# A two-layer trunk kernel on one core: from the framework's instruction scheduler to one written in the kernel

## The chip, the cores and the metric

The kernel runs on one core of a Trainium2 chip. The time is device time in microseconds (us) of one launch, lower is better. The engines of the core are named as in the profile: PE (TensorE, the matrix engine), DVE (VectorE), ACT (ScalarE), POOL (GpSimd) and SP (SyncE, which here issues every DMA). Each engine runs its own list of instructions strictly in order, and waits at an instruction until what that instruction needs is there.

## The reference

One sequence of 512 frames with 1024 features, led by 112 zero pads and 16 meta tokens, passes two layers and a last norm. Everything is float32.

```python
h = concat([zeros(112), meta_tokens(16), x(512)])          # 640 x 1024
# layer 0: w_in_ab (1024 x 4184)
aq, ak, av, ag, iq, ik, iw, bq, bk, bv, bg, ba = split(rms_norm(h, g0) @ w_in_ab)
oa = dsa_attention(...)       # indexer scores, top 128 keys of each query, softmax with a bias table
ob = gla_chunked(...)         # gated linear attention in chunks of 64
h += concat([oa * silu(ag), head_rms(ob) * silu(bg)]) @ w_out_ab
# layer 1: w_in_cd (1024 x 3584)
cq, ck, cv, cg, dq, dk, dv, dg = split(rms_norm(h, g1) @ w_in_cd)
oc = retention_chunked(rotary(cq), rotary(ck), cv)
od = stick_breaking(dq, dk, dv)      # softplus, reversed running sum, exp, times values
h += concat([head_layer_norm(oc) * silu(cg), od * silu(dg)]) @ w_out_cd
y = rms_norm(h[128:], final_g)
```

## The kernel before, in words

All state stays on the chip: the normalized sequence is held feature-major (128 features on the partitions, 528 positions: 16 meta tokens and 512 frames), and every projection is a sum over eight blocks of 128 features into a PSUM tile `acc` (two of them). To reach float32 accuracy each operand is split in two parts that the matrix engine takes: `hi` (line 135, on ACT) rounds it, `lo` (line 141, on DVE unless told otherwise) takes the remainder. A product is three matmuls (line 247): first part by first, second by first, first by second. The activations' parts are `hh` and `hl`, the weights' `wh` and `wl`.

Weights stream in. `load` (line 198) issues the DMA of the next 128x512 tile `raw` on SP; `split_next` makes `wh` on ACT and `wl` on DVE or, for three tiles in eight (`WPOOL = 3`), on POOL; five tiles are in flight. `COMB` is a projection whose weights are gathered from three places by three DMAs a half, over a tile that POOL zeroes first.

The projections are the matrix engine's stream, and everything else is laid beside them. Each branch is a Python generator (attention, the linear-attention heads, `stick_steps` at line 1220 and on, `retention_steps`, the norm) that does a little and yields; `tick` advances these generators between the products of a projection, with lags set by `LAG`. So the order in which the program states its work is already interleaved: `L1` and `L2` list the branches, V values, G linear attention, D the end of the top-k selection, A sparse attention, C its gate, S stick-breaking, R retention.

In the stick-breaking steps the chain of one unit is: scores on PE (line 460, `s`), a copy to SBUF (line 1246, DVE), absolute value, exp and log on ACT, a reversed running sum (line 1255, `TENSOR_TENSOR_SCAN`, DVE), a difference (1257, DVE), exp (1258, ACT), four transposes on PE (line 294, `tr<-ident,wt`), and the split of the turned tile into `pt` (135 on ACT, 141 on DVE) for the product with the values.

The order of the instructions on each engine is made by the framework's scheduler, which takes the program in the stated order and fills buffers with its own cost model; only `load_x`, the first stage, stands exactly as written (`manual_schedule`). Three PSUM banks serve both `s` and `tr` (the pool named `x` in the changed kernel), one serves `pv` (`y`), and rings of 8 and 10 SBUF buffers serve the tiles `st` and `wt`.

Of the kernel before, what the change touches and what calls it, by code (L numbers as in the profile page):

```python
# [9 lines left out]
F32 = mybir.dt.float32  # L10
# [6 lines left out]
P = 128  # L17
# [4 lines left out]
T = NMETA + SEQ  # L22
# [12 lines left out]
SROW = 656  # L35
# [4 lines left out]
    return slice(NMETA + P * b, NMETA + P * (b + 1))  # L40


class Kernel:
    def __init__(self, ctx, tc, ins, out):
        self.ctx, self.tc, self.nc = ctx, tc, tc.nc
        self.ins, self.out = ins, out
        nc = self.nc
        pool = lambda name, **k: ctx.enter_context(tc.tile_pool(name=name, bufs=1, **k))
# [5 lines left out]
        self.pp = pool("psum", space=bass.MemoryType.PSUM)  # L54
        self.dp = pool("scratch", space=bass.MemoryType.DRAM)
# [51 lines left out]
        return self.sm.tile(shape, F32, tag="mid", bufs=4, name=self.name("mid"))  # L107


    ST, WT, PT, GT = 8, 10, 8, 2  # L110
    RAW, WB = 5, 5


    WEVERY, WAHEAD, WPOOL = 1, 2, 3

    NL = (2, 5)

# [142 lines left out]
    def add(self, steps, wait=1, name=None):  # L260
        self.chains.append([self.now + wait, steps, name])
# [35 lines left out]
    def consts(self):  # L297
        nc, ins = self.nc, self.ins
        nc.scalar.preload_act_table_set("natural_log_exp_and_others")
        self.ident = self.cp.tile([P, P], F32, name="ident")  # L300
        make_identity(nc, self.ident)
# [46 lines left out]
    def load_x(self):  # L348
# [198 lines left out]
    def bias_steps(self):  # L547
        nc, ins = self.nc, self.ins
        rb = self.cp.tile([32, 8], F32, name="rb")
        nc.sync.dma_start(rb, ins["rel_bias"])  # L550
        oh = self.wt()
        oh2 = self.wt()
        nc.sync.dma_start(oh[:32, :512], ins["c_bucket"][:, :512])
        nc.sync.dma_start(oh2[:32, :SROW - 512], ins["c_bucket"][:, 512:])
        self.reps = []
        yield 8
        s1, s2 = self.s(), self.s()
        nc.tensor.matmul(s1[:8, :512], rb, oh[:32, :512], start=True, stop=True)
        nc.tensor.matmul(s2[:8, :SROW - 512], rb, oh2[:32, :SROW - 512], start=True, stop=True)
        r = self.wt()  # L560
        r2 = self.wt()
        nc.vector.tensor_copy(r[:8, :512], s1[:8, :512])
        nc.vector.tensor_copy(r2[:8, :SROW - 512], s2[:8, :SROW - 512])
        self.rows = self.dp.tile([8, SROW], F32, name="rows")
        nc.sync.dma_start(self.rows[:, :512], r[:8, :512])
        nc.sync.dma_start(self.rows[:, 512:], r2[:8, :SROW - 512])
        for h in range(8):
            t = self.dp.tile([P, SROW], F32, name=f"rep{h}")
            row = self.rows[h:h + 1, :]
            nc.sync.dma_start(t, bass.AP(tensor=row.tensor, offset=row.offset, ap=[[0, P], [1, SROW]]))  # L570
            self.reps.append(t)
        yield 1

    def strip(self, h):
        t = self.lt()
        row = self.reps[h][0:1, :]
        src = bass.AP(tensor=row.tensor, offset=row.offset + P - 1, ap=[[SROW - 1, P], [1, T]])
        self.nc.sync.dma_start(t, src)
        return t

# [752 lines left out]
    def play(self, parts, run):  # L1333
        for p in parts.split():
            run[p[0]](*(int(x) for x in p[1:]))

    def run(self):
        nc = self.nc
        self.consts()
        with self.tc.manual_schedule(engines={e.engine for e in (nc.tensor, nc.vector, nc.scalar, nc.gpsimd)}):  # L1340
            a, b = self.load_x()
        self.late_consts()
        self.add(self.bias_steps())
        self.indexer(a, b)
# [12 lines left out]
@with_exitstack  # L1357
# [63 lines left out]
```

## Time and profile before

| | us |
|---|---|
| median of three timed runs | 687.61 (687.45 to 688.51) |
| the profiled execution, its own time | 686.27 |
| its span, first to last instruction | 684.5 |
| PE busy in it | 644.6 (94%) |
| DVE busy | 485.1 (71%) |
| ACT busy | 386.1 (56%) |
| POOL busy | 150.9 (22%) |

The profile is of one execution. Times in it are in us from the start of the span. The stages, read off the first and last instruction of their lines: start and first norm 0 to 25, indexer and top-k with the values and the linear attention beside it 25 to 187, sparse attention 187 to 312, out-projection of layer 0 and the norm and values of layer 1 to 425, stick-breaking heads S0 and S1 425 to 486, retention R0 486 to 538, S2 and S3 538 to 600, R1 600 to 633, the last out-projection 633 to the end. An idle time that is put down to an engine's line is the time for which the waiting instruction's engine did nothing until that line's result came.

### The profile page before, as it was taken

To read this page: it belongs to the slowest core of one execution; us is meant where nothing else is said; L and a number is where in the kernel's file an instruction comes from. 1 tells how busy PE (TensorE), PEld (TensorE's weight loads), DVE (VectorE), ACT (ScalarE), POOL (GpSimd) and SP (SyncE) were. 2 spreads that over 40 slices of the span, in tenths; PEclk is the share of its full clock that TensorE was granted. 3 is DMA by queue.
4 is the path that set the end of the run, shared out by engine and by line. 5 is a ranking of instruction groups with operands and counts; after the bars stand their busy time and mean duration, and the time that the engine had idled before them with its cause. 6 is when DMAs were issued, how large, how long until landed. Compare 5 with 4: busy or idle time off the path is not lost.

```text
span 684.5 us, 12281 instructions
## 1 busy us (share of the span) xinstructions
PE 644.6 (94%) x4469; PEld 584.6 (85%) x4469; DVE 485.1 (71%) x1216; ACT 386.1 (56%) x846; POOL 150.9 (22%) x181
## 2 busy tenths in 40 slices
PE   8999998999999999999999999898899989799996
PEld 7879998989899999988898898777788778688784
DVE  5667899999968788798414635979635788935633
ACT  5656554252445747585435655888443798544434
POOL 6302211131131111020332221111221111310240
PEclk9999999999999999999999999999999999999999
DMA  8446223123124132112242642122222221313503
GB/s 231 109 106 200 60 59 93 47 79 104 36 80 110 47 94 63 47 48 78 79 126 60 200 126 78 32 77 62 63 63 66 58 62 47 94 47 97 186 25 123
DMA packets 91103, 59.25 MB, mean 87 GB/s; under 512 B 7314, under 2 KB 81628, under 8 KB 91044
## 3 DMA queue, kind: packets, MB, share of 16 engines
q1 hardware_dynamic: 91044, 58.48, 29.7%
q8 instruction: 35, 0.57, 0.3%
q14 instruction: 24, 0.20, 0.1%
HBM read 53.18 MB, written 6.90 MB: 88 GB/s over the span
## 4 chain that ended last, share of the span: by engine, by line
PE 54%; DVE 31%; ACT 10%; issue 3%; POOL 1%; DMA 0%; SPq 0%; ACTq 0%; DVEq 0%
PE acc L247 32%; PE tr L294 4%; DVE wt L1255 3%; PE acc L1295 3%; DVE m L536 3%; DVE lt L537 3%; DVE wl L141 3%; PE s L1295 2%; ACT st L135 2%; DVE wt L1257 1%; PE pv L683 1%; PE pv L684 1%; DVE wt L1091 1%; PE s L460 1%; DVE wt L1246 1%
## 5 line engine op out<-in xcount | busy, mean ns | idle before, releaser
L247 PE MATMUL acc<-hh,wh 128*128 128x272 f32 (+2 forms) x968 | 249.2, 317 | 3.0 <-ACT wt L610 1.0
L247 PE MATMUL acc<-hh,wl 128*128 128x272 f32 (+2 forms) x968 | 234.6, 302 | 1.3 <-POOL wl L141 1.3
L247 PE MATMUL acc<-hl,wh 128*128 128x272 f32 (+2 forms) x968 | 234.3, 303 | 0.7 <-DVE hl L143 0.7
L247 PEld LDWEIGHTS acc<-hh,wh 128*128 128x128 f32 x968 | 159.5, 191 | 11.9 <-issue 1.6
L135 ACT ACTIVATE wh<-raw 128x512 fp32r<-128x512 f32 x152 | 95.2, 628 | 131.1 <-PE acc L247 94.5
L247 PEld LDWEIGHTS acc<-hh,wl 128*128 128x128 f32 x968 | 159.0, 190 | 7.7 <-POOL wl L141 1.5
L247 PEld LDWEIGHTS acc<-hl,wh 128*128 128x128 f32 x968 | 158.6, 190 | 3.9 <-DVE hl L143 1.1
L141 POOL TENSOR_TENSOR wl<-raw,wh 128x512 fp32r<-128x512 f32 x58 | 76.1, 1311 | 344.2 <-ACT wh L135 314.4
L141 DVE TENSOR_TENSOR wl<-raw,wh 128x512 fp32r<-128x512 f32 x96 | 70.9, 741 | 37.0 <-ACT wh L135 32.8
L294 PE MATMUL tr<-ident,wt 128*128 128x128 f32 (+2 forms) x300 | 48.6, 282 | 10.1 <-DVE pt L141 5.9
L294 PEld LDWEIGHTS tr<-ident,wt 128*128 128x128 f32 (+2 forms) x300 | 35.1, 142 | 16.7 <-DVE pt L141 7.5
L460 PE MATMUL s<-st,st 128*128 128x272 f32 (+4 forms) x128 | 37.4, 304 | 5.3 <-DVE wt L1246 2.2
L135 ACT ACTIVATE st<-acc 64x528 fp32r<-64x528 f32 (+1 forms) x58 | 34.8, 599 | 1.7 <-PE acc L247 0.7
L747 POOL TENSOR_TENSOR gt<-gt,wt 128x528 f32<-128x528 f32 (+1 forms) x16 | 22.3, 1396 | 59.5 <-ACT wt L746 53.3
L460 PEld LDWEIGHTS s<-st,st 128*128 128x128 f32 x128 | 24.1, 188 | 11.9 <-issue 3.9
L537 DVE MATCH_REPLACE8 lt<-m,lt 128x144 f32<-128x144 f32 (+1 forms) x64 | 31.2, 492 | 0.1
L141 DVE TENSOR_TENSOR pt<-tr,pt 128x384 fp32r<-128x384 f32 (+1 forms) x48 | 27.9, 595 | 3.9 <-ACT pt L135 3.7
L1255 DVE TENSOR_TENSOR_SCAN wt<-wt,wt 128x144 f32<-128x144 f32 (+3 forms) x32 | 29.5, 942 | 1.6 <-ACT wt L1251 1.3
L536 DVE MAX8 m<-lt 128x8 f32<-128x144 f32 (+1 forms) x64 | 30.1, 498 | 0.6 <-POOL lt L530 0.4
L803 ACT ACTIVATE wt<-wt,tiny 128x144 f32<-128x144 f32 (+3 forms) x32 | 18.2, 571 | 19.4 <-DVE tiny L800 16.7
L683 PE MATMUL pv<-pt,vt 128*128 128x256 f32 x96 | 27.1, 283 | 0.0
L684 PE MATMUL pv<-pt,vt 128*128 128x256 f32 x96 | 26.9, 280 | 0.0
(247 smaller groups left out, 1093.7 us busy)
## 6 DMA issues: line engine op xcount, KB each, us to landing
raw<-in_w_in_ab_dram SPq DMA_DIRECT2D x64, 256.0 KB, 2.8
raw<-in_w_in_cd_dram SPq DMA_DIRECT2D x56, 256.0 KB, 2.9
raw<-in_w_out_ab_dram SPq DMA_DIRECT2D x16, 256.0 KB, 2.7
raw<-in_w_out_cd_dram SPq DMA_DIRECT2D x16, 256.0 KB, 2.6
rep<-rows SPq DMA_DIRECT2D x8, 328.0 KB, 6.9
lt<-rep SPq DMA_DIRECT2D x8, 264.0 KB, 2.9
pt<-in_x_dram SPq DMA_DIRECT2D x8, 256.0 KB, 4.4
wt<-in_x_dram SPq DMA_DIRECT2D x8, 256.0 KB, 4.0
```

What stands on the lines that cost most here:

```text
L135: self.nc.scalar.activation(out, src, AF.Copy, scale=1.0 if scale is None else scale)
L141: (eng or nc.vector).tensor_tensor(out, src, h, op=ALU.subtract)
L247: nc.tensor.matmul(a[:, c.start - c0:c.stop - c0], w[:, k % 4, :], x[:, k, c], start=k == order[0] and i == 0, stop=k == order[-1] and i == 2)
L294: self.nc.tensor.transpose(out, in_, self.ident[p0:p0 + n, p0:p0 + n])
L460: nc.tensor.matmul(out, q[:, qs], k[:, ks], start=True, stop=False)
L536: nc.vector.max(m8, sc)
L537: nc.vector.match_replace(sc, m8, sc, MARK)
L683: nc.tensor.matmul(dst, xh, pl, start=False, stop=False)
L684: nc.tensor.matmul(dst, xl, ph, start=False, stop=last and i == len(parts) - 1)
L747: nc.gpsimd.tensor_tensor(t[:, c], t[:, c], e[:, c], op=ALU.mult)
L1255: nc.vector.tensor_tensor_scan(mv[:, ::-1], mv[:, ::-1], lv[:, ::-1], 0.0, ALU.add, ALU.add)
L1295: nc.tensor.matmul(o[b], m[:, k, blk(b)], x, start=k == order[0] and i == 0, stop=k == order[-1] and i == 2)
```

## The change

The kernel's methods call the same instructions in the same stated order, but on recorders in place of the engines and the tile pools. `Recorder.add` notes each instruction with what it reads and writes, and gives it a cost from a table of fitted durations (`price`). After the whole program is recorded, `order` places all instructions with a list scheduler: in a loop, it offers for each engine one instruction that is ready (the one whose inputs come soonest, and of those that are there in time the one stated first; for PE an instruction counts as in time only when its inputs were there 300 ns before PE is free), takes the engine whose offer starts first, and gives out the buffers of each tag in the stated order. `issue` then emits the result with all five engines under `manual_schedule`, SP's DMAs among them.

Beside that, `WPOOL` goes from 3 to 0: all second parts `wl` but one go to DVE (57 instructions leave POOL), the rings grow (`st` 8 to 10, `wt` 10 to 12, `gt` 2 to 4), and the program is built with a smaller scratch for DMA descriptors. The arithmetic and the number of matmuls stay.

```diff
+    def add(self, eng, name, args, kw):
...
+        o.at = o.pri = len(self.ops)
...
+        for write, xs in ((False, ins), (True, outs)):
+            for x in xs:
+                self.depend(o, x, write)
+        self.price(o)
+        self.ops.append(o)
...
+    def price(self, o):
...
+        if o.eng == "tensor":
...
+            o.cost = max(273, 170 + 0.4375 * n) if not two else 180 + 1.62 * n
+        elif o.eng == "scalar":
+            o.cost = (205 if sbuf else 165) + 0.83 * n + (80 if isinstance(o.kw.get("bias"), View) or isinstance(o.kw.get("scale"), View) else 0)
...
+        elif o.eng == "vector":
+            o.port = sbuf and o.name not in ("max", "match_replace")
+            if o.name == "tensor_tensor_scan":
+                o.cost = 144 + 2.1 * n
...
+            else:
+                o.cost = 148 + 1.05 * n + scalar
...
+        elif o.eng == "gpsimd":
+            o.cost = {"memset": 92 + 0.84 * n, "tensor_tensor": 178 + 2.17 * n}.get(o.name, 194 + 1.5 * n)
+        else:
...
+            o.cost = 2000 + kb * (9 if any(y.tile.whole for y in o.outs + o.ins) else 3.5)
+    LAT = {"tensor": 55, "vector": 33, "scalar": 34, "gpsimd": 60, "sync": 27}
+    OVER = {"vector": -84, "scalar": -103, "gpsimd": -60}
+    SWITCH, ROWS = 86, 50
+    MARGIN = 300
...
+    def order(self):
...
+        while left:
+            best = None
+            for e, xs in lists.items():
+                pick = None
+                base = free[e] + (last.mm[2] if e == "tensor" and last is not None else 0)
+                for o in xs:
+                    est = o.est
+                    ok = True
+                    for t in o.tiles:
+                        if t.slot:
+                            continue
+                        k = t.kind
+                        if t.at != k.next or not k.free:
+                            ok = False
+                            break
+                        est = max(est, min(k.free)[0] + self.LAT[e])
+                    if not ok:
+                        continue
+                    now = free[e] + (self.slot(last, o) if e == "tensor" and last is not None else 0)
+                    start = max(est, now)
+                    key = (max(est + (self.MARGIN if e == "tensor" else 0) - base, 0.0), o.pri)
+                    if pick is None or key < pick[0]:
+                        pick = (key, start, o)
+                if pick and (best is None or pick[1] < best[1]):
+                    best = pick
...
+            if e == "vector" and o.port and begun.get("pool", (0, 0))[0] < start < begun.get("pool", (0, 0))[1] - 100:
+                cost += begun["pool"][1] - start - 70
...
+    def issue(self):
+        todo = self.order()
...
+        with self.tc.manual_schedule(engines=engines):
+            for o in todo:
...
+                getattr(getattr(self.core, o.eng), o.name)(*[bind(x) for x in o.args],
+                                                           **{k: bind(x) for k, x in o.kw.items()})
...
-    ST, WT, PT, GT = 8, 10, 8, 2
-    RAW, WB = 5, 5
+    ST = 10
+    WT = 12
+    PT = 8
+    GT = 4
...
-    WEVERY, WAHEAD, WPOOL = 1, 2, 3
+    WPOOL = 0
...
-        with self.tc.manual_schedule(engines={e.engine for e in (nc.tensor, nc.vector, nc.scalar, nc.gpsimd)}):
-            a, b = self.load_x()
+        a, b = self.load_x()
...
+        nc.issue()
...
+                     dynamic_dma_scratch_size=1024)
```

In the changed kernel every instruction is issued from line 373, so its rows all show that line. PE before, at the end of S1, near 484 us: `acc_1201` is the value projection of R0, `tr_1215` the bank into which the last unit's weights (`wt_1186`) are turned.

```order
3107 L247 MATMUL acc_1201_6373<-hh_799_4221,wl_1190_6307 128x272
3108 L247 MATMUL acc_1201_6373<-hh_799_4221,wl_1190_6307 128x256
3109 L294 MATMUL tr_1215_6451<-ident_76,wt_1160_6174 128x128
3110 L294 MATMUL tr_1205_6404<-ident_76,pm_1146_6105 32x128
3111 L294 MATMUL tr_1215_6451<-ident_76,wt_1186_6293 128x128
3112 L294 MATMUL tr_1215_6451<-ident_76,wt_1160_6174 128x128
3113 L294 MATMUL tr_1215_6451<-ident_76,wt_1186_6293 128x128
3114 L247 MATMUL acc_1201_6373<-hh_799_4221,wh_1189_6306 128x272
```

PE in the changed kernel at the same place: `acc_58` is the gate projection that follows that value projection, `x_238` the bank of the same transposes, `wt_195` the last unit's weights.

```order
3127 L373 MATMUL acc_58_6463<-hl_3_4254,wh_110_6196 128x512
3128 L373 MATMUL acc_58_6463<-hh_3_4242,wl_110_6253 128x512
3129 L373 MATMUL acc_58_6463<-hh_3_4242,wh_111_6242 128x512
3130 L373 MATMUL x_238_6497<-ident_76,wt_187_6291 128x128
3131 L373 MATMUL x_238_6497<-ident_76,wt_195_6420 128x128
3132 L373 MATMUL x_238_6497<-ident_76,wt_187_6291 128x128
3133 L373 MATMUL x_238_6497<-ident_76,wt_195_6420 128x128
3134 L373 MATMUL x_235_6366<-ident_76,pm_7_6235 32x128
3135 L373 MATMUL acc_58_6463<-hl_3_4254,wh_111_6242 128x512
```

The last part of the value projection and the first part of the gate's, 25 matmuls, now stand ahead of the last unit's transposes. Near the end of S3 it is the same with the projections of R1.

ACT before, in the first norm: `hh` are the first parts of the first blocks of the sequence, made of the turned input `s`.

```order
12 L135 ACTIVATE hh_2_135<-s_39_221,gains_132 128x272
13 L135 ACTIVATE hh_2_135<-s_40_227,gains_132 128x272
14 L135 ACTIVATE hh_2_135<-s_42_234,gains_132 128x272
15 L377 ACTIVATE wt_44_241,tiny_43_240<-pt_13_156 128x512
16 L135 ACTIVATE hh_2_135<-s_46_249,gains_132 128x272
```

ACT in the changed kernel at the same place: `wh_4` and `wh_5` are the first parts of the two halves of `COMB`, made of `raw_4` and `raw_5`.

```order
15 L373 ACTIVATE hh_2_324<-x_4_272,gains_84 128x272
16 L373 ACTIVATE hh_2_324<-x_5_274,gains_84 128x272
17 L373 ACTIVATE tiny_9_315<-tiny_9_315,eps_83 128x1
18 L373 ACTIVATE tiny_9_315<-tiny_9_315 128x1
19 L373 ACTIVATE wh_4_347<-raw_4_232 128x512
20 L373 ACTIVATE wh_5_357<-raw_5_242 128x512
21 L373 ACTIVATE hh_2_324<-x_6_351,gains_84 128x272
22 L373 ACTIVATE hh_2_324<-x_7_360,gains_84 128x272
```

Two splits of weights now stand ahead of the fourth and later `hh`.

SP in the changed kernel, where the DMAs of those two tiles stand among the constants (before, the three DMAs of each tile stood together, ahead of all constants):

```order
18 L373 DMA w2_98<-in_gla_gate_w2_dram 16x256
19 L373 DMA tri_99<-in_c_tri_dram 128x128
20 L373 DMA strict_100<-in_c_strict_dram 128x128
21 L373 DMA raw_4_232<-in_w_in_ab_dram 128x4x8
22 L373 DMA raw_5_242<-in_w_in_ab_dram 128x4x8
23 L373 DMA dmat_101<-in_c_dmat_dram 128x512
24 L373 DMA raw_7_309<-in_w_in_ab_dram 128x4x128
25 L373 DMA zeta_102<-in_c_zeta_dram 128x8
26 L373 DMA raw_4_232<-in_w_in_ab_dram 128x4x16
27 L373 DMA raw_5_242<-in_w_in_ab_dram 128x4x16
```

The third DMA of each tile has moved behind five DMAs of constants and two other weight tiles.

## Rows read from the trace of the kernel before

**Rows 1.** Page, busy time: engine, us, share of the span, instructions
```profile
PE 644.6 (94%) x4469; PEld 584.6 (85%) x4469; DVE 485.1 (71%) x1216; ACT 386.1 (56%) x846; POOL 150.9 (22%) x181
```

**Rows 2.** Windows: stretch, length, PE, PEld, DVE, ACT, POOL busy, clock, DMA, GB/s
```profile
75.00:187.00 112.00, 106.21 (x833) 101.06 (x832) 108.09 (x334) 48.47 (x111) 23.37 (x33) 0.98 0.27 69
187.00:312.00 125.00, 121.04 (x969) 116.76 (x968) 101.17 (x324) 78.31 (x182) 22.57 (x20) 1.00 0.25 67
...
425.00:486.00 61.00, 53.56 (x340) 45.39 (x339) 55.65 (x115) 48.14 (x96) 13.57 (x11) 0.99 0.23 66
486.00:538.00 52.00, 52.00 (x327) 45.49 (x327) 22.94 (x42) 23.66 (x48) 7.66 (x6) 0.98 0.21 59
538.00:600.00 62.00, 54.29 (x343) 46.17 (x342) 56.18 (x117) 48.69 (x99) 13.26 (x11) 0.98 0.21 62
```

**Rows 3.** Waits of PE, 425 to 600: us in total, times, longest
```profile
PE tr L294 <- DVE pt L141: 5.1, 2, 2.7
PE tr L294 <- DVE wt L1246: 3.6, 6, 1.2
...
PE s L460 <- DVE pt L141: 1.3, 4, 0.4
```

**Rows 4.** Timeline, two ends of a stick stretch: start, us, engine, instruction, [idle before]
```profile
480.35 1.58 POOL L141 TENSOR_TENSOR wl<-raw,wh 128x512 fp32r<-128x512 f32 x1 [1.07 <-ACT wh L135]
480.72 2.33 DVE L1255 TENSOR_TENSOR_SCAN wt<-wt,wt 128x528 f32<-128x528 f32 x1
...
484.91 0.48 PE L294 MATMUL tr<-ident,wt 128*128 128x128 f32 x1 [2.35 <-DVE pt L141]
...
594.30 1.25 DVE L1255 TENSOR_TENSOR_SCAN wt<-wt,wt 128x528 f32<-128x528 f32 x1
```

**Rows 5.** Timeline of PE, two neighbours of a projection
```profile
429.74 0.40 PE L247 MATMUL acc<-hl,wh 128*128 128x512 f32 x1
429.98 0.39 PE L247 MATMUL acc<-hh,wl 128*128 128x512 f32 x1
```

**Rows 6.** Window of 3.4 us behind a stall of PE (columns as rows 2)
```profile
597.30:600.70 3.40, 3.18 (x15) 2.89 (x15) 2.27 (x6) 2.47 (x6) 0.61 (x1) 0.50 0.00 0
```

**Rows 7.** Instructions on `wl`: page (POOL), line 141 (DVE, min/median/max ns)
```profile
L141 POOL TENSOR_TENSOR wl<-raw,wh 128x512 fp32r<-128x512 f32 x58 | 76.1, 1311 | 344.2 <-ACT wh L135 314.4
...
L141 DVE TENSOR_TENSOR wl<-raw,wh x96: 655/691/1725, 18.3 to 664.8; 128x512 fp32r<-128x512 f32 x96
```

**Rows 8.** Windows, `wl` on POOL alone: stretch, length, POOL busy (x)
```profile
75.00:187.00 112.00, 12.13 (x10) 0.98 0.27 69
187.00:312.00 125.00, 13.40 (x11) 1.00 0.25 67
425.00:486.00 61.00, 6.86 (x5) 0.99 0.23 66
```

**Rows 9.** Waits of PE, 75 to 312
```profile
PE tr L294 <- DVE attm L969: 3.1, 3, 2.0
...
PE tr L294 <- DVE tiny L791: 0.8, 2, 0.5
```

**Rows 10.** Waits of PE, 312 to 425
```profile
PE tr L294 <- ACT wt L1116: 1.3, 2, 0.7
```

**Rows 11.** Last selection step, first step of attention that uses it: min/median/max, first, last start
```profile
L536 DVE MAX8 m<-lt x64: 280/495/712, 74.4 to 186.7; 128x8 f32<-128x144 f32 x16, 128x8 f32<-128x272 f32 x16, 128x8 f32<-128x400 f32 x16, 128x8 f32<-128x528 f32 x16
...
L785 DVE TENSOR_TENSOR wt<-lt,lt x32: 286/501/1659, 202.1 to 313.7; 128x144 f32<-128x144 f32 x8, 128x272 f32<-128x272 f32 x8, 128x400 f32<-128x400 f32 x8, 128x528 f32<-128x528 f32 x8
```

**Rows 12.** Timeline of the start, ACT and SP's queue
```profile
13.88 0.49 ACT L135 ACTIVATE hh<-s,gains 128x272 fp32r<-128x272 f32 x1 [1.66 <-PE s L294]
...
18.89 0.63 ACT L135 ACTIVATE wh<-raw 128x512 fp32r<-128x512 f32 x1
...
15.49 0.43 SPq L320 DMA_DIRECT2D zeta<-in_c_zeta_dram  x1
```

**Rows 13.** Page, DMA issues: KB each, us from issue to landing
```profile
raw<-in_w_in_ab_dram SPq DMA_DIRECT2D x64, 256.0 KB, 2.8
```

More of the change, by code (lines that the diff above doesn't have):

```diff
@@ L40, in blk, with __init__, __getitem__, __getattr__ @@
     return slice(NMETA + P * b, NMETA + P * (b + 1))
+class View:
+    __slots__ = ("tile", "chain", "real")
+    def __init__(self, tile, chain, real):
+        self.tile, self.chain, self.real = tile, chain, real
+    def __getitem__(self, k):
+        return View(self.tile, self.chain + (("__getitem__", (k,), {}),), self.real[k])
+    def __getattr__(self, name):
+        got = getattr(self.real, name)
+        if name not in ("rearrange", "unsqueeze", "broadcast_to", "bitcast"):
+            return got
+        return lambda *a, **k: View(self.tile, self.chain + ((name, a, k),), got(*a, **k))
+    def other(self, fn):
+        return View(self.tile, (("", fn, None),), fn(self.real))
+    def bind(self):
+        x = self.tile.shaped(self.tile.buf)
+        for name, a, k in self.chain:
+            x = a(x) if name == "" else getattr(x, name)(*a, **k)
+        return x
+    def region(self):
+        t = self.tile
+        if t.whole:
+            return 0, 1, 0, 1
+        x = self.real
+        ap, off = [list(y) for y in x.ap], x.offset
+        width = t.width
+        p0, c0 = off // width, off % width
+        lo = c0 + sum(min(0, st * (n - 1)) for st, n in ap[1:])
+        hi = c0 + sum(max(0, st * (n - 1)) for st, n in ap[1:]) + 1
+        if t.psum:
+            return 0, P, 0, t.width
+        return p0, p0 + ap[0][1], lo, hi
+    def free(self):
+        n = 1
+        for y in self.real.shape[1:]:
+            n *= y
+        return n
@@ new lines, with __init__, shaped @@
+class Held:
+    def __init__(self, kind, shape, dt, psum, whole):
+        self.kind, self.shape, self.dt, self.psum, self.whole = kind, list(shape), dt, psum, whole
+        self.buf, self.slot, self.left, self.ends = None, None, 0, 0.0
+        self.log, self.fixed = [], False
+    def shaped(self, buf):
+        if self.fixed:
+            return buf
+        n = 1
+        for y in self.shape[1:]:
+            n *= y
+        x = buf[:self.shape[0], :n]
+        if x.dtype != self.dt:
+            x = x.bitcast(self.dt)
+        if len(self.shape) > 2:
+            names = "abcd"[:len(self.shape) - 1]
+            x = x.rearrange(f"p ({' '.join(names)}) -> p {' '.join(names)}", **dict(zip(names, self.shape[1:])))
+        return x
@@ new lines, with __init__, buffer, tile @@
+class Kind:
+    def __init__(self):
+        self.free, self.made, self.next, self.n = [], 0, 0, 0
+    def buffer(self, i, dt):
+        self.n += 1
+        return self.pool.tile([P, self.width], dt, tag=f"{self.tag}_{i}", bufs=1, name=f"{self.tag}_{self.n}")
+class RecordedPool:
+    def __init__(self, rec, pool, psum=False, whole=False):
+        self.rec, self.pool, self.psum, self.whole = rec, pool, psum, whole
+        self.kinds = {}
+    def tile(self, shape, dt, tag=None, bufs=1, name=None):
+        fixed = tag is None
+        tag = tag or name
+        n = 1
+        for y in shape[1:]:
+            n *= y
+        if tag not in self.kinds:
+            k = self.kinds[tag] = Kind()
+            width = max(n, {"tiny": 32, "mid": P}.get(tag, 0))
+            k.width, k.pool, k.tag = width, self.pool, tag
+            k.free = [(0.0, i) for i in range(bufs)]
+            k.any = self.pool.tile(shape, dt, name=tag) if fixed else k.buffer(0, F32)
+        k = self.kinds[tag]
+        t = Held(k, shape, dt, self.psum, self.whole)
+        t.width = k.width
+        if fixed:
+            t.fixed, t.buf = True, k.any
+        return View(t, (), t.shaped(k.any))
@@ new lines, with __init__, __getattr__ @@
+class Op:
+    __slots__ = ("eng", "name", "args", "kw", "outs", "ins", "tiles", "preds", "succs", "wait", "est", "at", "cost",
+                 "mm", "port", "pri", "begin", "end")
+class RecordedEngine:
+    def __init__(self, rec, name, engine):
+        self._rec, self._name, self._engine = rec, name, engine
+    def __getattr__(self, op):
+        if op in ("preload_act_table_set", "engine"):
+            return getattr(self._engine, op)
+        return lambda *a, **k: self._rec.add(self._name, op, a, k)
@@ L43 @@
 class Kernel:
     def __init__(self, ctx, tc, ins, out):
-        self.ctx, self.tc, self.nc = ctx, tc, tc.nc
+        self.ctx, self.tc, self.nc = ctx, tc, Recorder(tc)
         self.ins, self.out = ins, out
         nc = self.nc
-        pool = lambda name, **k: ctx.enter_context(tc.tile_pool(name=name, bufs=1, **k))
+        pool = lambda name, psum=False, whole=False, **k: RecordedPool(
+            self.nc, ctx.enter_context(tc.tile_pool(name=name, bufs=1, **k)), psum, whole)
         self.cp = pool("const")
@@ L53, in __init__ @@
         self.sm = pool("small")
-        self.pp = pool("psum", space=bass.MemoryType.PSUM)
-        self.dp = pool("scratch", space=bass.MemoryType.DRAM)
+        self.pp = pool("psum", True, space=bass.MemoryType.PSUM)
+        self.dp = pool("scratch", False, True, space=bass.MemoryType.DRAM)
         self.n = 0
@@ L107, in mid @@
         return self.sm.tile(shape, F32, tag="mid", bufs=4, name=self.name("mid"))
-    ST, WT, PT, GT = 8, 10, 8, 2
-    RAW, WB = 5, 5
-    WEVERY, WAHEAD, WPOOL = 1, 2, 3
+    ST = 10
+    WT = 12
+    PT = 8
+    GT = 4
+    RAW = 5
+    WB = 5
+    WEVERY = 1
+    WAHEAD = 2
+    WPOOL = 0
     NL = (2, 5)
@@ L300, in consts @@
         self.ident = self.cp.tile([P, P], F32, name="ident")
-        make_identity(nc, self.ident)
+        make_identity(nc.core, self.ident.real)
         warm = self.pv()
@@ L568, in bias_steps @@
             t = self.dp.tile([P, SROW], F32, name=f"rep{h}")
-            row = self.rows[h:h + 1, :]
-            nc.sync.dma_start(t, bass.AP(tensor=row.tensor, offset=row.offset, ap=[[0, P], [1, SROW]]))
+            nc.sync.dma_start(t, self.rows.other(lambda x, h=h: bass.AP(
+                tensor=x[h:h + 1, :].tensor, offset=x[h:h + 1, :].offset, ap=[[0, P], [1, SROW]])))
             self.reps.append(t)
@@ L575, in strip @@
         t = self.lt()
-        row = self.reps[h][0:1, :]
-        src = bass.AP(tensor=row.tensor, offset=row.offset + P - 1, ap=[[SROW - 1, P], [1, T]])
+        src = self.reps[h].other(lambda x: bass.AP(
+            tensor=x[0:1, :].tensor, offset=x[0:1, :].offset + P - 1, ap=[[SROW - 1, P], [1, T]]))
         self.nc.sync.dma_start(t, src)
@@ L1408 @@
     from concourse.bass_utils import run_bass_kernel_spmd as _run
-    nc = _bacc.Bacc("TRN2", target_bir_lowering=False, num_devices=1)
+    nc = _bacc.Bacc("TRN2", target_bir_lowering=False, num_devices=1,
+                     dynamic_dma_scratch_size=1024)
     arrays, aps = {}, {}
```

138 lines of the change are left out of this document (added).

## The prediction

> **What bounds the kernel now.** I read the busy times first. PE is busy for 644.6 of 684.5 us, and no other engine comes near it [rows 1]. The number of matmuls stays, so the change can only win what PE does not work: 684.5 - 644.6 = 39.9 us, or lose by adding to it. An average says nothing on where that idle time lies, so the windows by stage came next, in which the reader is to compare the busy time of PE with the length of the stretch [rows 2]. The two stick-breaking stretches hold 61 - 53.56 = 7.44 and 62 - 54.29 = 7.71 us, 15.15 in all. The indexer, top-k and attention stretches (75 to 312) hold 5.79 + 3.96 = 9.75. In R0, between the two stick stretches, PE never stops: 52.00 of 52. The rest lies in the norm, the start and the end.
>
> The third view is that of the waits, for what ends the idle time. In the stick stretches it is DVE nearly every time: the copies of the scores, and the splits of the turned weights into `pt`, two of which cost 2.7 and 2.4 us [rows 3]. The timeline shows one of these: the transposes on PE wait 2.35 us until 484.91, and the scan on DVE, which began at 480.72, is the long step of the chain that they wait for [rows 4]. PE runs its list in order, so the projections of R0, whose inputs are long there, stand behind it.
>
> **The change part by part.** A, the stick stretches. The scheduler passes over an instruction whose inputs are late and takes the matmuls of the next projection. At both places 25 of them now come ahead of the transposes: fifteen of 256 or 272 columns, ten of 512. Neighbours of 512 columns start 429.98 - 429.74 = 0.24 us apart [rows 5], those of about half the columns then 0.125 (an estimate by columns), so 10 x 0.24 + 15 x 0.125 = 4.3 us of work fill a stall, which is longer than the stall. The smaller waits on the copies of the scores get up to a few matmuls as well.
>
> How much comes of it is decided by DVE, which is busy for 55.65 of 61 us there [rows 2], and which also gets five more `wl` in each of the two stretches (five on POOL in the first, and as many in the other) [rows 8]. One costs 0.69 us on DVE, the median [rows 7], so 5 x 0.69 = 3.45. Against that stands what DVE loses now while POOL works: the scan took 2.33 us beside the `wl` on POOL that began at 480.35, and 1.25 where none ran, 1.08 more [rows 4]. If each of five `wl` on POOL stretches one instruction so, 5.4 come back; if none, 0; I take the middle, 2.7. DVE then has 55.65 + 3.45 - 2.7 = 56.4 us in the first stretch and 56.18 + 0.75 = 56.9 in the second. At 98% busy (above the 108.09 of 112, 96.5%, that it reaches in the top-k now) that is 57.6 and 58.1. The stretch becomes 3.4 and 3.9 shorter, and the 4.3 of the next stage's matmuls are done within it: 7.7 + 8.2 = 15.9. From PE's side it is the 15.15 of idle time. I take **-15.5**. The bounds: nothing, if the passed-over transposes come late in turn; and on the other side the idle time, plus what a stop costs beyond it, since the last matmul before a stop runs 0.40 where its neighbour would have started at 0.24 [rows 5], 0.16 on each of the 12 waits of rows 3, so 1.9; plus the half clock. Behind each of the two long stalls PE ran at a granted clock of 0.50 (the 1.2 GHz level) for 3.4 us [rows 6], and the work in it would have taken half of that: 2 x 1.7 = 3.4. Together 20.5.
>
> On these stretched instructions the trace can be set against the Trainium skill, "SBUF — State Buffer", section "SBUF: two separate sides": a VectorE instruction with two SBUF inputs and a GpSimd instruction that reads SBUF take one port pair in turn, and the loser stands still until the other has ended. The scan of 2.33 us agrees in its size, since POOL's `wl` ended at 481.93, 1.25 us more is 483.18, and the scan ended at 483.05. By that rule each of the 57 moved `wl` could have held DVE for up to 1.3 us and costs 0.69 now, so DVE would become lighter, and part A would go to its bound of 20.5.
>
> B, 75 to 312. The waits there are DVE's too: 3.1 us on the masked scores of the linear attention and some short ones [rows 9]; the new order puts 3 to 14 matmuls ahead of the transposes that wait on the attention's normalizer and `pt`, and nothing ahead of the longest, 2.0. Of the 9.75 idle I count 3 as filled, **-3**; 5 at most. The price is on DVE: 21 `wl`, ten of them before 187 and eleven after [rows 8], 21 x 0.69 = 14.5. In the top-k the selection steps show no stretching (712 ns for the longest `MAX8` over 528 columns [rows 11]), so I count no relief there: 108.09 + 6.9 = 115.0 of 112, 3.0 over. It is hidden because the selection's last step begins at 186.7 and its first user at 202.1 [rows 11]: 15.4 us in hand. From 187 on, half of 11 x 1.08 comes back, 5.9, and DVE has 101.17 + 7.6 - 5.9 = 102.9 of 125. If that cover is gone, 14.5 - 5.9 = 8.6 are added: bounds -5 to +8.6.
>
> C, the norm. Two waits on ACT, 1.3 us [rows 10], get 12 and 6 matmuls ahead of them: **-1.3**, between 0 and -1.6 (with 0.16 for each stop).
>
> D, the start. On ACT two `wh` of `COMB` now stand ahead of the fourth `hh`, and wait for DMAs that SP issues about where it issues `zeta` now, at 15.49 [rows 12]. A weight tile lands 2.8 us after its issue [rows 13]: 18.3, then two `wh` of 0.63, 19.5, where that `hh` began at 13.88 [rows 12]: 5.6 us late. But before, ACT had no more to do with the first weights until 18.89, so the end of the stage need not slip by all of it. Bounds 0 and +5.6; I take **+1.5**, nearer to the lower end because the later `hh` waited for PE's transposes of the second half anyway.
>
> What else changes costs nothing that I can name: the larger rings only let work start earlier, POOL is left at 22% or less, and the DMA share lies under 0.3 in the stages in question [rows 2].
>
> The sum: -15.5 - 3 - 1.3 + 1.5 = -18.3. Against the profiled execution's 686.27 that is 668.0; the median of the runs stands 687.61 - 686.27 = 1.3 above it, so **669 us**.
>
> **The rivals.** *Better (656).* All that the orders could win is won: A 20.5, B the whole 9.75, C 1.6, D nothing, 31.9 less: 654.4 + 1.3. For it: DVE gets lighter if POOL's stretching was the reason for its late results. Against: the order of the changed kernel has nothing ahead of the longest wait of rows 9, and the chains in front of the small waits are as long as before.
>
> *Half (681).* The transposes that were passed over come later by up to the 4.3 us put ahead of them, and their banks and `pt` come free later; the scores of the next unit, which need a bank of the same three, then wait. Half of A is given back, B and C are nothing: -7.7 + 1.5 = -6.2, 680.1 + 1.3. For it: the waits of PE are on just-in-time results, and a plan on fitted durations that is off by a few hundred ns puts the stop elsewhere. Against: fifteen of the 25 matmuls belong to a projection which is finished anyway before the transposes matter.
>
> *Names only (687).* The framework's scheduler had the same stated order, and most of PE's list is the same, so the new places may lie where DVE sets the end anyway: 55.65 of 61 us leaves DVE little idle time. Against: the stalls of 2.35 to 2.7 us lie behind DVE's chain, not in front of it.
>
> *Slower (692).* DVE becomes the bound. No stretching goes away (POOL's rows and DVE's long scans only happened together), and from 75 to 312 all of the 14.5 us of added `wl` lands on the path, because matmuls wait for a `wl` that stands behind selection steps in DVE's list. In the stick stretches DVE then has 59.1 and 59.6, at 98% 60.3 and 60.8, and A is 0.7 + 1.2 + 8.6 = 10.5. Sum: +14.5 - 10.5 - 1.3 + 1.5 = +4.2, 690.5 + 1.3. It decides from the point where more than 10.3 of the 14.5 are on the path. Against: DVE is idle for 3.9 + 23.8 = 27.7 us in 75 to 312 [rows 2].
>
> The Trainium skill, "Perfetto Trace Analysis", section "Optimizing Scalar/DVE Operations", speaks for this rival: when VectorE is saturated, moving work from it to GpSimd may be worth it, though the shared port can eat the gain. Here the work goes the other way, onto an engine at 96.5% in one stretch [rows 2]. By its first half the top-k stretch should grow; by its second nothing is lost. No row of before decides between the two.
>
> **How the numbers follow.** My forecast 0.42 (its own range 660 to 677), better 0.17, half 0.21 (677 to 686), names only 0.08, slower 0.12. Two runs of this kernel differ by 0.15% and more, so under 0.2% (1.4 us) counts as no change: faster 0.42 + 0.17 + 0.21 = 0.80, same 0.08, slower 0.12. The range 651 to 686 leaves out the slower case, about half of names only, and 0.03 below.
>
> **What would show it.** Right: in the profile after, PE is busy for 98% in the stretch around S0 and S1 and in that around S2 and S3, no wait of PE there is over 1 us, and the half clock behind the two stalls is gone; the scans of 528 columns are near 1.25 us each; DVE's busy time as a whole rises by less than 57 x 0.69 = 39 us, since some of it is paid back. The top-k's last step starts some 3 us later, with no new wait of PE behind it. At the start ACT waits for a `raw`, and the first projection begins some 1.5 us later. Wrong: PE waits for a `wl` made on DVE anywhere between 75 and 312 (the slower case); or the stick stretches keep their idle time with waits on a bank or `pt` in other places (half); or the list of PE is as fast in the stretch but its next stage starts with the same wait.

## The result, and the profile after

The changed kernel takes 670.02 us (median of four runs, 667.77 to 671.61) against 687.53 for the kernel before on the same chip: a ratio of 0.9751, 95% interval 0.9706 to 0.9796, so 17 us or 2.5% less. The profiled execution took 667.77, with a span of 666.0 where it was 684.5.

The busy times of the page, as [rows 1]: engine, us, share, instructions.

```profile
PE 635.4 (95%) x4469; PEld 580.6 (87%) x4469; DVE 507.4 (76%) x1273; ACT 383.1 (58%) x846; POOL 74.9 (11%) x124
```

DVE gained 57 instructions and 507.4 - 485.1 = 22.3 us, not the 39 that 57 times 0.69 come to; POOL's busy time fell by 76.0 us. PE does the same 4469 matmuls in 9 us less of busy time, part of which is the clock (below).

The stretches of the changed kernel that hold the same work on PE as those of [rows 2] from 75 to 312 and the two of stick-breaking, in the same columns:

```profile
74.70:307.40 232.70, 225.17 (x1800) 216.40 (x1799) 217.31 (x678) 126.84 (x292) 18.89 (x32) 1.00 0.27 72
...
418.30:479.00 60.70, 56.72 (x367) 49.24 (x366) 56.80 (x122) 50.25 (x103) 6.27 (x6) 1.00 0.22 62
524.90:586.00 61.10, 57.77 (x361) 50.81 (x360) 56.16 (x120) 48.97 (x101) 6.26 (x6) 0.94 0.21 59
```

The last two are as long as before and hold more work: 367 and 361 matmul records where there were 340 and 343. PE is busy for 93 to 95% of them, not for 98%. From 74.7 to 307.4 DVE is now busy for 93% of the time, and PE's idle time is 7.5 us where it was 9.75.

The waits of PE from 418 to 595, as [rows 3] (us in total, times, longest); then, for the scans of [rows 4], the group of all eight scans of 528 columns (busy us, mean ns).

```profile
PE x L373 <- DVE wt L373: 4.5, 7, 1.7
...
PE x L373 <- DVE pt L373: 0.4, 1, 0.4
```

```profile
L373 DVE TENSOR_TENSOR_SCAN wt<-wt,wt 128x528 f32<-128x528 f32 x8 | 10.0, 1253 | 0.5 <-ACT wt L373 0.5
```

The stops of 2.4 and 2.7 us on `pt` at the ends of the two stretches are gone, 5.1 us down to 0.4. The eight scans last 1.25 in the mean. A new wait of 1.7 us stands earlier in each stretch, on the copies of the scores (`wt`). On the timeline the first one ends just behind such a copy, which reads scores out of a PSUM bank of the pool `x`; the transposes that wait write into such a bank.

```profile
461.77 0.42 DVE L373 COPY wt<-x 128x272 f32<-128x272 f32 x1
...
462.25 0.55 PE L373 MATMUL x<-ident,wt 128*128 128x128 f32 x3 [1.65 <-DVE wt L373]
```

To see where the 18.5 us of span went, I numbered the 2904 matmul records of the projections into `acc` ahead of the last out-projection (from 0) and compared the start of the one with the same number in each trace, at four places, with the end of the span behind them:

| matmul into `acc` | before | changed | own order, POOL keeps its share | framework's order, all on DVE | changed, longer lag |
|---|---|---|---|---|---|
| 271st | 75.1 | 74.7 | 77.6 | 75.2 | 75.8 |
| 1545th | 312.1 | 307.4 | 313.7 | 310.4 | 309.0 |
| 2183rd | 425.1 | 418.3 | 426.2 | 422.7 | 419.9 |
| 2593rd | 538.1 | 524.9 | 534.8 | 531.4 | 524.0 |
| end | 684.5 | 666.0 | 676.0 | 672.7 | 659.7 |

By this the start gave 0.4 us, the stretch to the 1545th 4.2, the norm 2.2, and all that follows, the stick-breaking with R0, R1 and the end, 11.7.

### The profile page after: what moved, and what is told of

It is laid out like the page before. It is cut to its first block, busy times and chain, and to the rows that moved or that the text cites. A ratio compares the mean times of both kernels' runs of the same rounds, so it can differ in the third digit from the quotient of the medians.

```text
span 666.0 us, 12243 instructions
## 1 busy us (share of the span) xinstructions
PE 635.4 (95%) x4469; PEld 580.6 (87%) x4469; DVE 507.4 (76%) x1273; ACT 383.1 (58%) x846; POOL 74.9 (11%) x124
## 4 chain that ended last, share of the span: by engine, by line
PE 68%; DVE 17%; ACT 9%; issue 3%; DMA 1%; SPq 1%; POOL 0%; POOLq 0%; ACTq 0%; DVEq 0%
PE acc L373 46%; PE x L373 15%; PE y L373 6%; ACT wt L373 4%; DVE wt L373 3%; DVE lt L373 3%; DVE m L373 3%; DVE st L373 3%; DVE wl L373 2%; ACT st L373 2%; ACT wh L373 1%; SPq L373 1%; DVE pt L373 1%; DMA pt<-in_x_dram 1%; ACT pt L373 1%
## 5 line engine op out<-in xcount | busy, mean ns | idle before, releaser
L373 DVE TENSOR_TENSOR wl<-raw,wh 128x512 fp32r<-128x512 f32 x153 | 111.0, 732 | 50.9 <-ACT wh L373 49.7
L373 PE MATMUL x<-ident,wt 128*128 128x128 f32 (+2 forms) x300 | 48.1, 278 | 7.7 <-DVE wt L373 4.5
L373 PE MATMUL x<-st,st 128*128 128x272 f32 (+6 forms) x240 | 50.9, 290 | 0.6 <-DVE pt L373 0.4
L373 ACT ACTIVATE wt<-x 128x272 f32<-128x272 f32 (+3 forms) x68 | 29.3, 434 | 34.3 <-PE x L373 22.4
L373 ACT ACTIVATE wt<-wt 128x528 f32<-128x528 f32 (+3 forms) x74 | 43.0, 593 | 9.2 <-DVE wt L373 8.4
L373 PEld LDWEIGHTS x<-ident,wt 128*128 128x128 f32 (+2 forms) x300 | 34.5, 140 | 15.5 <-DVE wt L373 6.7
L373 PEld LDWEIGHTS x<-st,st 128*128 128x128 f32 (+2 forms) x240 | 37.8, 187 | 6.5 <-DVE pt L373 1.3
L373 PE MATMUL y<-pt,vt 128*128 128x256 f32 (+1 forms) x288 | 39.7, 281 | 0.0
L373 PEld LDWEIGHTS y<-pt,vt 128*128 128x128 f32 x288 | 37.7, 195 | 0.1
L373 DVE TENSOR_TENSOR_SCAN wt<-wt,wt 128x64 f32<-128x64 f32 (+5 forms) x50 | 29.9, 634 | 1.1 <-ACT wt L373 1.0
```

Source lines behind the costliest of these rows:

```text
L373: getattr(getattr(self.core, o.eng), o.name)(*[bind(x) for x in o.args], **{k: bind(x) for k, x in o.kw.items()})
```

## The experiments

Each ratio is that of the timed runs to the kernel before, with its 95% interval.

**The order alone.** The changed kernel keeps POOL's share of the `wl`.

```diff
-    WPOOL = 0
+    WPOOL = 3
```

> The changed kernel with WPOOL = 3, so that 58 second parts stay on POOL and only the order and the rings change. Theory 1 (the prediction's: PE's list has work ahead of the waiting transposes): nearly all of the gain stays, 668 to 675 us, at most 5 us lost because POOL stretches scans again (VectorE busy 485 plus or minus 5 us instead of 507). Theory 2 (the gain is VectorE's relief from POOL): at least 10 us come back, 680 us or more. Rival 3 (the second parts on VectorE cost time that the order has to win back): faster than the changed kernel, 660 to 667.

678.61 us, 0.9875 (0.9842 to 0.9908). Between the theories: by the medians half of the gain is left, and 8.6 us hang on where the `wl` are made, so theory 1 falls for the whole program. For the stick stretches it holds: from the 2183rd `acc` matmul to the end this kernel takes 676.0 - 426.2 = 249.8 us, 9.6 less than before, and the changed kernel 11.7 less. Its waits of PE from 425 to 605 and its scans:

```profile
PE x L373 <- DVE wt L373: 4.5, 8, 0.8
...
PE x L373 <- DVE pt L373: 0.6, 3, 0.2
```

```profile
L373 DVE TENSOR_TENSOR_SCAN wt<-wt,wt 128x528 f32<-128x528 f32 x8 | 10.0, 1250 | 0.0
```

The two stops on `pt` are gone with POOL's `wl` still there, and the scans are as short as in the changed kernel: the new order alone has kept POOL clear of these scans. Of the 10.0 us by which the profiled span exceeds that of the changed kernel, 7.9 are lost ahead of the 2183rd matmul, and 6.5 of the 10.0 are PE's clock (last section).

**The move alone.** The kernel before, all `wl` but one on DVE, the framework's scheduler.

```diff
-    WEVERY, WAHEAD, WPOOL = 1, 2, 3
+    WEVERY, WAHEAD, WPOOL = 1, 2, 0
```

> The kernel before with WPOOL = 0: the second parts go to VectorE, the framework's scheduler keeps the order and the rings. Theory 1: within 4 us of before, 683 to 691, with the 2.4 and 2.7 us stops of PE at the ends of the stick stretches still there. Theory 2: 670 to 677. The prediction's slower case (VectorE becomes the bound from 75 to 312): 692 or more, with waits of PE on a second part made on VectorE.

676.51 us, 0.985 (0.9828 to 0.9872): theory 2's number. One constant of the old kernel is worth 10.7 us. Its timeline at the place of [rows 4], and its waits of PE from 416 to 590:

```profile
476.87 1.25 DVE L1255 TENSOR_TENSOR_SCAN wt<-wt,wt 128x528 f32<-128x528 f32 x1
...
479.98 0.33 PE L294 MATMUL tr<-ident,wt 128*128 128x128 f32 x1 [0.89 <-DVE pt L141]
```

```profile
PE tr L294 <- DVE pm L1260: 2.1, 3, 1.0
PE tr L294 <- DVE pt L141: 1.8, 2, 0.9
```

The two stops fell from 5.1 to 1.8 us. The framework now puts four more matmuls of 256 and 272 columns ahead of the first of these transposes, some 0.5 us at the 0.125 of the prediction; the rest is DVE's chain in front of them, which got shorter, as the scan shows. At the other stop the scan had not been stretched before (594.30 in [rows 4]), but the instruction ahead of it on DVE. Before, on POOL and DVE, and in this kernel on DVE:

```profile
592.44 1.38 POOL L141 TENSOR_TENSOR wl<-raw,wh 128x512 fp32r<-128x512 f32 x1 [1.73 <-ACT wh L135]
592.60 1.77 DVE L1133 TENSOR_TENSOR st<-st,wt 128x512 f32<-128x512 f32 x1
```

```profile
584.10 0.68 DVE L1133 TENSOR_TENSOR st<-st,wt 128x512 f32<-128x512 f32 x1
```

1.77 - 0.68 = 1.09, on the chain as well. In the whole trace PE waits for no `wl` made on DVE, and the 1545th `acc` matmul is 1.7 us early and not late: the slower rival is refuted.

**What of the move does it.** `fw_dve`, and POOL makes the 57 subtractions a second time, for nobody; then the same with two memsets in place of each subtraction.

```diff
-        self.lo(wl, raw, wh, eng=nc.gpsimd if pool else nc.vector)
+        self.lo(wl, raw, wh, eng=nc.gpsimd if self.nw <= self.PL else nc.vector)
+        if pool and self.nw > self.PL:
+            junk = self.wp.tile([P, 512], F32, tag="junk", bufs=1, name=self.name("junk"))
+            nc.gpsimd.tensor_tensor(junk, raw, wh.bitcast(F32), op=ALU.subtract)
```

> The kernel before with the second parts on VectorE (as in fw_dve), and POOL makes the same 57 subtractions of 128x512 once more into a tile that nobody reads. Theory 2a (POOL's reading stretches VectorE's instructions, and that is what the move takes away): the gain of fw_dve is gone, 684 to 692 us, the scans of 528 columns last 1.35 us or more in the mean, and the stops of PE at the ends of the stick stretches are over 2 us again. Theory 2b (a second part is simply there 0.6 us sooner from VectorE than from POOL): it stays at 674 to 679, whatever POOL does.

> As fw_junk (framework's order, second parts on VectorE), but POOL's extra work is two memsets of 128x512 for each of the 57 tiles: about as long, and it reads nothing. If POOL's reading of SBUF is what stretches VectorE: the gain of fw_dve stays, 674 to 680 us, scans of 528 columns near 1.25 us. If any work of POOL that writes SBUF does it: 690 or more, scans stretched as in fw_junk.

With the subtractions: 697.52 us, 1.0156 (1.0136 to 1.0177), 5 us beyond what was expected. PE's list is that of `fw_dve`, matmul for matmul (all 4469, by tiles and shapes). The busy times of the page, the stop's scan with POOL's instruction, the group of the scans, and the waits of PE from 430 to 615:

```profile
PE 652.0 (93%) x4469; PEld 590.8 (85%) x4469; DVE 531.5 (76%) x1273; ACT 385.8 (55%) x846; POOL 165.0 (24%) x181
```

```profile
493.17 1.54 POOL L217 TENSOR_TENSOR junk<-raw,wh 128x512 f32<-128x512 f32 x1 [1.12 <-issue]
493.48 2.34 DVE L1258 TENSOR_TENSOR_SCAN wt<-wt,wt 128x528 f32<-128x528 f32 x1
```

```profile
L1258 DVE TENSOR_TENSOR_SCAN wt<-wt,wt 128x528 f32<-128x528 f32 x8 | 12.2, 1524 | 0.4 <-ACT wt L1254 0.4
```

```profile
PE tr L297 <- DVE pt L141: 5.1, 2, 3.1
PE tr L297 <- DVE wt L1249: 4.9, 6, 1.3
```

The same 1273 DVE instructions take 26.4 us more than the 505.1 of `fw_dve`, 0.46 for each subtraction on POOL; the scan takes 2.34 us as in [rows 4]; the two stops are back at 5.1 us. Theory 2b falls, since a `wl` comes from DVE here too.

With the memsets: 685.75 us, 0.9978 (0.996 to 0.9996); the expectation of 674 to 680 was missed. The rows are the memsets (one of two lines: min, median, max ns, first and last start), the `wl` on DVE from 20 to 91, and two of the waits of PE in the whole trace:

```profile
L217 POOL MEMSET junk<- x57: 518/525/723, 20.1 to 89.6; 128x512 f32 x57
```

```profile
L141 DVE TENSOR_TENSOR wl<-raw,wh x18: 673/692/695, 21.6 to 86.8; 128x512 fp32r<-128x512 f32 x18
```

```profile
PE tr L298 <- POOL junk L217: 5.7, 1, 5.7
...
PE tr L298 <- DVE pt L141: 2.5, 3, 0.9
```

The memsets wait for no data and ran early in POOL's list: all 114 lie between 20.1 and 90.7 us, and the first scan of 528 columns starts at 448.3. So the edit did not put its question to the scans, and that they last 1.25 us here answers nothing. Most of the loss against `fw_dve` is an accident of the same kind, since PE once waits 5.7 us for POOL, near 89 us: the 648th matmul into `acc` is 8.6 us late against before, and the 2875th 0.2. Between these two this kernel wins 8.4 us; `fw_dve` goes from 2.8 early to 11.5 early, 8.7.

The trace answers part of the question at another place. The 18 subtractions `wl` on DVE of the row above all ran beside the memsets, and none lasted over 0.695 us; of the 44 that overlap a repeated subtraction on POOL in the kernel of 697.52 us, 19 lasted 0.72 to 1.79. So what stretches DVE's subtraction of two SBUF tiles is POOL's work that reads, and not POOL's work that only writes; for the scans that is inferred, not shown. This is what the Trainium skill says in "SBUF — State Buffer", section "SBUF: two separate sides": VectorE with two SBUF inputs conflicts only with a GpSimd instruction that reads SBUF. The traces agree for `wl`, 0.69 us in the mean beside the memsets and 0.98 beside the subtractions. Writing isn't free for every instruction: one `TENSOR_SCALAR` of DVE (`lt<-wt,iw`, 128x528) lasts 0.73 us beside two memsets and 0.50 in `fw_dve`.

**PE in the stated order; the others in the stated order.** Two edits to the scheduler: for the engines in question only the next stated instruction is offered. Below is the first; the second does the same for the four other engines.

```diff
+        stated = [o.at for o in ops if o.eng == "tensor"] + [-1]
...
+                if e == "tensor":
+                    xs = [o for o in xs if o.at == stated[0]]
                 for o in xs:
...
+            if e == "tensor":
+                stated.pop(0)
```

> The changed kernel, but PE's list keeps the stated order; the other four engines are still placed by the kernel's scheduler. Theory 1: the stops in the stick stretches are back (PE idle 13 us or more there, against 8.1 in the changed kernel), 680 to 690 us. Rival 3 (the order of VectorE and ACT is what counts, since the chain in front of the transposes is theirs): 668 to 675.

> The changed kernel, but only PE's list is reordered; ACT, VectorE, POOL and SP keep the stated order. Theory 1: most of the gain stays, 668 to 678. Rival 3: as slow as before or slower, 686 or more, with waits of PE on VectorE everywhere.

731.59 (1.0653, 1.0626 to 1.068) and 850.11 us (1.2373, 1.234 to 1.2406). Both far outside: the stated order was never what ran before. The framework's scheduler reorders every engine as well, so neither run undoes the change, and they only say that reordering is worth far more than the difference of the two schedulers. A better undoing is the next one.

**How far PE passes over.**

```diff
-    MARGIN = 300
+    MARGIN = -2000
```

> The changed kernel with MARGIN = -2000: PE keeps to the stated first instruction even where its inputs come up to 2 us later, and passes over it only beyond that. Theory 1 (the matmuls put ahead of the waiting transposes are what the order wins): stops of 1 to 2 us come back, most of all in the stick stretches, 677 to 690 us. If the order wins elsewhere: 668 to 673.

> The changed kernel with MARGIN = 0: an instruction of PE counts as in time when its inputs come just as PE is free. If durations miss by some hundred ns, stops of 0.2 to 0.5 us appear before transposes that were timed exactly: 671 to 677. If the margin only delays the chain: 664 to 668.

693.86 us (1.0092, 1.0069 to 1.0116) with -2000, and 674.83 (0.982, 0.9792 to 0.9849) with 0. Waits of PE with -2000, whole trace:

```profile
PE x L373 <- DVE pt L373: 12.4, 16, 2.6
PE x L373 <- DVE wt L373: 6.8, 17, 0.9
PE x L373 <- DVE attm L373: 4.6, 3, 1.9
```

In the changed kernel these groups are 5.3, 4.5 and 2.5 us. So passing over late transposes is what the order lives on: without it, the rest of the scheduler kept, the kernel is 0.9% slower than before. The loss is larger than expected (24 us, not 7 to 20) and lies in all stages: the 1545th `acc` matmul starts 11.7 us later than in the changed kernel (319.1), the span ends 26.0 later (692.0). That says more than the prediction did, since the framework's order passes over late work as well, and `fw_dve` is faster than this. With 300 ns the median is 5 us lower than with 0, but the two intervals touch (0.9796 and 0.9792), and by the mean granted clock of the timed runs (0.983 and 0.978) some 3 of the 5 us are PE's clock: what the margin itself is worth isn't shown.

**The rings.** `st` 8, `wt` 10, `gt` 2, as before.

```diff
-    ST = 10
-    WT = 12
+    ST = 8
+    WT = 10
...
-    GT = 4
+    GT = 2
```

> The changed kernel with the rings of before (st 8, wt 10, gt 2). If the larger rings only let work start earlier and cost nothing else, as the prediction has it: 668 to 673, the same within 2 us. If the new order needs them to run ahead: 675 or more, with waits of ACT or VectorE for a free wt.

670.48 us, 0.9763 (0.9745 to 0.9782): the same as the changed kernel. The rings give nothing.

**A better version.** The two stops of 1.7 us left come where PE reaches a unit's transposes before DVE is done.

```diff
-    LAG = {"a": 5, "d": 6, "t": 1, "v": 4, "n": 9, "s": 6, "k": 11}
+    LAG = {"a": 5, "d": 8, "t": 1, "v": 4, "n": 9, "s": 6, "k": 11}
```

> The changed kernel with LAG d = 8 in place of 6: in the stated order a stick unit's transposes come two steps later, behind more matmuls of a projection. If what is left in the stick stretches is PE arriving too early at the last unit's transposes (stops of 1.65 us near 461 and 567): these stops fall under 1 us, 663 to 668 us. If VectorE's chain sets the end of a unit whatever stands ahead: 669 to 673, with the same stops somewhat later.

> The kernel before with the second parts on VectorE and LAG d = 8: the two constants that did well, under the framework's scheduler. If the longer lag is worth as much here as under the kernel's own order (8 us): 667 to 671, the new scheduler then being worth some 6 us more. If the framework's order has already put as much ahead of the transposes: 674 to 679, the same as fw_dve.

Under the kernel's own order: 662.03 us, 0.9645 (0.9622 to 0.9669), 8 us better than the changed kernel and a little beyond the expected 663. PE in the two stretches of sticks, and its waits from 418 to 590:

```profile
419.90:480.00 60.10, 57.99 (x377) 50.83 (x376) 55.67 (x119) 49.20 (x102) 6.28 (x6) 1.00 0.23 66
524.00:585.00 61.00, 59.58 (x393) 52.46 (x392) 57.89 (x122) 50.88 (x106) 6.25 (x6) 1.00 0.25 72
```

```profile
PE x L373 <- DVE pt L373: 1.2, 4, 0.4
PE x L373 <- DVE st L373: 0.8, 1, 0.8
PE x L373 <- DVE wt L373: 0.8, 3, 0.3
```

No wait is over 0.8 us, and PE is busy for 96.5 and 97.7%: what the prediction had expected of the changed kernel itself. Under the framework's order the same two constants give 680.58 us, 0.9915 (0.9894 to 0.9936), worse than the move alone: 4.5 us of waits appear on `pm`, and a scan takes 1.46 us in the mean. So the longer lag pays only under the new scheduler.

## Why the prediction was right

The time was forecast at 669 and came at 670; the sum, 18.3 us less, at 18.5 by the profiled spans. That it fits so well is luck: A gave 3.8 us less than forecast, and B, C and D together 4.0 more.

A, forecast -15.5, measured -11.7 from the 2183rd matmul to the end. This is the mis-sized term. Of the 25 matmuls ahead of the transposes, six of 256 or 272 columns had stood there before, so 19 are new: 10 x 0.24 + 9 x 0.125 = 3.5 us for a stall, not 4.3. The step that failed most is "at 98% busy": DVE came to 56.80 of 60.70 and 56.16 of 61.10, 94 and 92%; a stop of 1.7 us came up in each stretch, at other transposes than those that the prediction looked at waiting for a copy that frees a bank (a sign of "half"); and behind one of them PE ran 6.8 us at half its clock (below), 3.4 us lost. The relief of DVE was mis-sized too: I took 0.54 us for each moved `wl` (2.7 for five); over the program it was (39.3 - 22.3)/57 = 0.30.

By the Trainium skill's rule on the port pair ("SBUF — State Buffer", "SBUF: two separate sides") I had set up to 1.3 us for each beside that. The mean is far below, 0.30 here and 0.46 in `fw_junk`; single instructions do lose 1.1.

The mechanism of A was right, but it was not the only one. I booked the win to PE's list and the moved `wl` as a cost that nearly pays for itself. By the table, from the 2183rd matmul to the end the order alone wins 9.6 us, the move alone 9.4 (250.0 where 259.4 were) and both 11.7: either does most of it, and they largely do the same. Over the whole program the medians give the order alone 687.18 - 678.61 = 8.6 us and the move alone 687.18 - 676.51 = 10.7, 19.3 together where both give 17.5, but PE's clock has a large share in these two numbers (last section). The stop behind the scan of 2.33 us in [rows 4] was the clue: that scan is the long step of the chain *because* of POOL, and I used the 1.08 us only in DVE's sum of busy time, where 2.7 more or less hardly count. On the chain, it is latency: the two stops fell from 5.1 to 1.8 us, of which new matmuls ahead of them account for 0.5 in each. A stall that a chain sets is to be priced by the chain's stretched steps, not by the engine's share.

B, forecast -3, measured -4.2. Some 1.7 of it is clock, an estimate: before, PE ran the 3.4 us from 122.8 to 126.2 at a granted clock of 0.51, and in the changed kernel that stage has 1.00; the prediction counted nothing for that. DVE's busy time rose by 217.3 - 209.3 = 8.0 for 21 `wl`, against my 14.5 - 5.9 = 8.6. The top-k ended later as forecast, without harm: its last step in the changed kernel (min, median, max, first and last start) is 3.5 us later than in [rows 11], 3.0 were forecast, and nobody waits for it.

```profile
L373 DVE MAX8 m<-lt x64: 289/496/711, 75.1 to 190.2; 128x8 f32<-128x144 f32 x16, 128x8 f32<-128x272 f32 x16, 128x8 f32<-128x400 f32 x16, 128x8 f32<-128x528 f32 x16
```

C, forecast -1.3, measured -2.2; more than the waits of [rows 10], so something other than these two waits gave 0.9, which I did not trace.

D, forecast +1.5, measured -0.4 by the 271st matmul. ACT does wait for `raw` ahead of the fourth `hh`, as forecast. But the projection is late before that, since the transposes in front of the first `hh` wait on PE for the norm's chain until 13.75:

```profile
17.43 1.15 ACT L373 ACTIVATE wh<-raw 128x512 fp32r<-128x512 f32 x2 [1.51 <-DMA raw<-in_w_in_ab_dram]
```

```profile
13.75 0.90 PE L373 MATMUL x<-ident,pt 128*128 128x128 f32 x3 [2.62 <-DVE pt L373]
```

Its first matmul starts at 14.90 (10.85 before). That wait of 2.62 us the prediction didn't have. Of the 4.1 us, 0.6 are left at the 15th matmul and nothing at the 21st. The end of the range that took the delay as hidden was the right one; what hides it I did not test.

The rival "names only" is refuted by `own_pool3`, "slower" by `fw_dve`. "Half" (681) had its sign in part, the two waits of 1.7 us for a bank, and not its time. "Better" wanted 20.5 in A and 31.9 in all: the longer lag reaches (684.5 - 425.1) - (659.7 - 419.9) = 19.6 in A, and 24.8 in all.

## What to carry to other kernels

Where the slowest engine waits at the end of a chain, compare each step of the chain with its shortest sibling of the same shape: a step that takes twice as long names a disturber, and moving that work can be worth as much as a better order in the stage where it stands, with one constant. Two remedies for one stall should be tried apart and together before either is given the credit. An in-order engine gains from passing over late instructions, and how far work is stated ahead (`LAG`) must be tuned again after a change of scheduler: the same number gave 8 us under one and cost 4 under the other.

## What was not expected of the hardware

PE's clock. In the changed kernel PE ran at the lower level, 0.50 granted (1.2 GHz), at the start (12.2 to 19.0), at the end, and once between. That one stood behind a stop, but not each stop had such a sequel: two stops of 1.65 and 1.68 us, at the same point of the two stretches, differed. Behind the one that ended at 567.98 (columns as in [rows 2]):

```profile
568.40:575.20 6.80, 6.04 (x29) 5.77 (x28) 6.69 (x15) 4.29 (x10) 0.00 (x0) 0.51 0.24 67
```

Behind the one that ended at 462.25 the clock stayed at full speed: the stretch 418.30 to 479.00 above has 1.00.

Over a whole trace, the time at the lower level adds up to 18.9 us before, 15.5 in the changed kernel, 11.5 in `fw_dve` and 28.5 in `own_pool3`. Half of it counted as lost, an estimate that takes PE to set the pace throughout, that is 9.4, 7.8, 5.7 and 14.2. So 6.5 of the 10 us by which the spans of `own_pool3` and the changed kernel differ is clock in these two executions.

The medians don't average this out. By the mean granted clock of the timed runs (0.983 before, 0.983 in the changed kernel, 0.988 in `fw_dve`, 0.974 in `own_pool3`) the loss is 11.2, 11.5, 8.0 and 17.5 us. With it left out, by the same estimate (rather too much where PE waits anyway), the order alone wins 14.9 us, the move alone 7.6 and both 17.1. So the median of the order alone hides some 6 us of what it saves, and of the 8.6 us that the move seems to add to it 2.2 are left. Whether the order alone brings that clock about by its own stops is open. Which stops bring the lower level was not settled.
